# Turns of the cached K rows in layer 1: later places in the order, behind the additions of products

## The chip, the cores and the metric

The kernel runs on one core of a Trainium2 chip. The metric is the device time of one execution in microseconds (us), as the median of several runs. Beside the timed runs stands one execution that was recorded by the hardware profiler; all times inside the kernel come from it. Its engines are named PE (TensorE: matmuls, with PEld for the loads of its stationary operand), DVE (VectorE), ACT (ScalarE), POOL (GpSimd) and SP (SyncE, which here only issues DMAs).

## The reference

A trunk of two layers over a prompt of 512 tokens and a sample group of 8 sequences with 16 new tokens each (640 rows of 1024). Layer 0 is a gated MLP and is not touched. Layer 1 projects q, k, v and z for 16 heads of 128, lets the prompt attend to itself and the sample rows attend to 256 cached rows and themselves, with a bias from cumulative forget values, and gates the result with silu(z). For the sample group:

```python
k = jnp.concatenate([k_cache.astype(k_new.dtype), k_new], axis=1)
v = jnp.concatenate([v_cache.astype(v_new.dtype), v_new], axis=1)
s = jnp.einsum('bqhd,bkhd->bhqk', q, k).astype(jnp.float32) * scale
s = s + cT[:, :, P:, None] - cT[:, :, None, :]
s = jnp.where(mask, s, -jnp.inf)
p = jax.nn.softmax(s, axis=-1).astype(v.dtype)
return jnp.einsum('bhqk,bkhd->bqhd', p, v).reshape(B, T, H * dh)
```

The cached K (8 sequences, 256 rows, 16 heads, 128 values, f32) must stand transposed in memory, with the 128 values on the partitions, before the scores can be computed.

## The kernel before, in words

**Work on PE.** Every f32 matrix is split into a high and a low part, and a product is three matmuls (`mm3`, lines 271 to 273). The projections of layer 1 use Strassen's scheme of seven products for a 2 by 2 block (`seven_products`, from line 556): each of the seven has four `mm3` with 320 columns and ends in one of four PSUM banks. The first product is copied out by ScalarE (line 571); VectorE adds the others to partial sums (lines 573, 575, 578), and four times an addition completes a quarter of the output (`total`, line 562). PE can run ahead of these additions only as far as banks are free.

**Layer 1.** Heads are worked on in eight pairs. The loop over p from 0 to 6 runs four projections in each pass: z of pair p, then v, k and q of pair p+1, 28 `mm3` each. `interleave` counts 0.441 for each `mm3`, so that a projection is 12.35 and a pass 49.4 of its units, and puts the pieces of attention in at given times: scores, turn, values and gate of the prompt heads (`prompt_times`) and of two groups of four sample sequences (`sample_times`), and the loads and turns of cached data. The last pair's attention is spread over project_z(7) and the first half of the output projection (`out_steps` in `tail`).

**Cached K.** `load_k(p, bg, hh)` brings the rows of one head hh of pair p for one group bg of four sequences, 512 KB, into `kraw` by four DMAs of 128 KB, one for each quarter of 32 partitions, issued by SP (line 124). It puts 32 by 32 blocks where they are to be turned. `turn_k(p, bg, hh)` turns them with four transposes on VectorE (line 1051) into `kt[:, hh]`. There is one `kraw` and one `kt` for the two heads: a load can start only when the turn before it has read `kraw`, and a turn can write `kt` only when the sample scores of the group before have read it. `new_k` adds the new rows to `kt` (GpSimd, line 1055). Then the scores of the group are computed on PE (line 1073). A pair has four turns: group 0 head 0, group 0 head 1, group 1 head 0, group 1 head 1; each is followed by the load for the next.

**What sets the order.** The program is traced in the order that `interleave` gives, and the framework then orders the instructions of each engine itself: it runs the program through a simulated timeline and lets an instruction whose operands are ready there pass others that were traced before it. On the chip each engine then works its list off in that order, so an instruction that waits holds up what stands behind it. `queued(...)` limits this: every instruction traced inside it on the named engine is ordered behind the instruction kept in `behind`, without a wait of its own. `behind["dve"]` is set by `total`, so in layer 1 it is the latest traced addition that completed a quarter of a projection.

**Other DMAs of a pass.** SP also issues the loads of cached V, the stores of k (16 DMAs, behind the transposes of `store_k`, line 920) and v (5), the masks and biases and two stores of y. The weights of layer 1 are loaded by GpSimd's queue (line 122).

Of the kernel before, what the change touches and what calls it, by code (L numbers as in the profile page):

```python
# [32 lines left out]
PAST = 256  # L33
# [24 lines left out]
def hybrid_trunk(tc, x_prompt, x_sample, ck, cv, clf, p_prompt, p_sample, norm_pre, norm_post,  # L58
                 g_win, ln_g, ln_b, w_s, b_s, g_wout, f_win, b_f, f_wout, w_proj, w_gate, consts,
                 y_p, y_s, st_v, fk_p, fv_p, fl_p, fk_s, fv_s, fl_s):  # L60
    nc = tc.nc
# [28 lines left out]
    def r1(o, n, p=P):  # L90
        return R1[:p, o:o + n]
# [11 lines left out]
    def bank(lst=(0, 1, 2, 3, 4, 5, 6, 7)):  # L103
        return PB[ring(("bank", lst), lst)]
# [15 lines left out]
    def dma(out, in_, queue=None):  # L120
        if queue is not None:
            queue.dma_start(out=out, in_=in_)
        else:
            behind["sp"] = nc.sync.dma_start(out=out, in_=in_)  # L124

    @contextmanager
    def queued(*engines):

        with ExitStack() as stack:
            for e in engines:  # L130
                stack.enter_context(tc.issue_after(behind[e].ins))
            yield
# [223 lines left out]
    def interleave(steps, pieces):  # L356


        now, todo = 0.0, sorted(pieces, key=lambda x: x[0])
        for took in steps:  # L360
            now += took
            while todo and todo[0][0] <= now:
                todo.pop(0)[1]()
        for _, piece in todo:
            piece()
# [97 lines left out]
    for p in range(4):  # L463
# [3 lines left out]
        out = [bank((0, 1, 2, 3, 4, 5, 6, 7)) for _ in range(NT)]  # L467
# [88 lines left out]
    def seven_products(into, done, partial=None):  # L556

        m1, u2, u3 = partial or (into(0, 0), into(0, 1), into(1, 0))
        rights = (quarter(0, 0), right_sum(1), quarter(0, 1), right_sum(0), quarter(1, 1), quarter(1, 0), right_sum(2))

        def total(i, j, a, b):
            behind["dve"] = nc.vector.tensor_tensor(out=into(i, j), in0=a, in1=b, op=ALU.add)  # L562
            done(i, j, into(i, j))

        for n, (w, right) in enumerate(zip(seven_left(), rights)):
            o = bank(UZ)[:, :HT]
            for k in range(4):
                mm3(o, (w[0][:, k], w[1][:, k]), (right[0][:, k], right[1][:, k]), k == 0, k == 3)
                yield 0.441
            if n == 0:  # L570
                nc.scalar.activation(out=m1, in_=o, func=AF.Copy)
            elif n == 1:
                nc.vector.tensor_tensor(out=u2, in0=m1, in1=o, op=ALU.add)
            elif n == 2:
                nc.vector.tensor_tensor(out=u3, in0=u2, in1=o, op=ALU.add)  # L575
            elif n == 3:
                total(1, 1, u3, o)
                nc.vector.tensor_tensor(out=u2, in0=u2, in1=o, op=ALU.add)
            elif n == 4:
                total(0, 1, u2, o)  # L580
            elif n == 5:
                total(0, 0, m1, o)
            else:
                total(1, 0, u3, o)
# [276 lines left out]
    def both(o, i):  # L861
        return r1(o + i * TOK, TOK)
# [7 lines left out]
    def kn_of(h):  # L870
        return both(o_k, h % 2)[:, 512:]
# [29 lines left out]
    def turn_v(p, i):  # L901

        v = v_of(p)
        b = bank(ATT)
        for t in range(4):
            nc.tensor.transpose(out=b[:, t * P:(t + 1) * P], in_=both(o_vk, i)[:, t * P:(t + 1) * P], identity=ident)
        nc.scalar.activation(out=v[:, :4, i * P:(i + 1) * P], in_=b.rearrange("p (t n) -> p t n", t=4), func=AF.Copy)
        if i:
            b = bank(ATT)
            for z in range(2):  # L910
                nc.tensor.transpose(out=b[:, z * P:(z + 1) * P], in_=both(o_vk, z)[:, 512:], identity=ident)
            nc.scalar.activation(out=v[:, 4], in_=b[:, :256], func=AF.Copy)
            for t in range(NT):
                store_v(p, t)
# [30 lines left out]
    def project_q(p):  # L945

        def done(i, j, c):
            if j == 1:
                nc.scalar.activation(out=qpads[:, i, :, i, :], in_=both(o_q, i)[:, 512:].rearrange("p (b q) -> p b q", b=NB), func=AF.Copy)

        yield from seven_products(lambda i, j: both(o_q, i)[:, HALF[j]], done)

    def project_z(p):

        def done(i, j, c):
            th = r1(o_vk + 3 * HT, HT)
            nc.scalar.activation(out=th, in_=c, func=AF.Tanh, scale=0.5)
            nc.vector.scalar_tensor_tensor(out=c, in0=th, scalar=1.0, in1=c, op0=ALU.add, op1=ALU.mult)

        yield from seven_products(lambda i, j: both(o_z, i)[:, HALF[j]], done, [r1(o_vk + z * HT, HT) for z in range(3)])  # L960

    def project(*parts):
        for part in parts:
            yield from part
# [3 lines left out]
    def w0_of(h):  # L968
        return tri if h % 2 else SF[:, 2048:2560] if h < 14 else r1(o_raw, 512)

    def load_w0(h):
        dma(w0_of(h), c_sc[h].partition_broadcast(P))
# [59 lines left out]
    kraw = r1(o_K, 1024).rearrange("p (b n) -> p b n", b=4)  # L1032
    kt = r1(o_KT, 2176).rearrange("p (h b k) -> p h b k", h=2, b=4)
    vv = r1(o_V, 2048).rearrange("p (b t n) -> p b t n", b=4, t=2)

    def load_k(p, bg, hh):
        for qd in range(4):
            d = slice(qd * 32, (qd + 1) * 32)
            dma(kraw[d].rearrange("p b (c d) -> p (b c) d", d=32),
                ck[0, 4 * bg:4 * bg + 4, :, 2 * p + hh, d].rearrange("b (c j) d -> j (b c) d", j=32))  # L1040

    def load_v(p, bg):
        for z in range(2):
            b = 4 * bg + 2 * z
            dma(vv[:, 2 * z:2 * z + 2].rearrange("p b t n -> p (b t) n"),
                cv[0, b:b + 2, :, 2 * p:2 * p + 2, :].rearrange("b (t k) h d -> k (b t) (h d)", k=P))

    def turn_k(p, bg, hh):

        for bl in range(4):  # L1050
            nc.vector.transpose(out=kt[:, hh, bl, :PAST], in_=kraw[:, bl])  # L1051

    def new_k(p, bg):
        for hh in range(2):
            nc.gpsimd.tensor_copy(out=kt[:, hh, :, PAST:], in_=kn_of(2 * p + hh)[:, 64 * bg:64 * bg + 64].rearrange("p (b k) -> p b k", b=4))
# [61 lines left out]
    def prompt_times(h, t0, step):  # L1117

        setup, scores, turn, values = prompt_pieces(h)
        res = [(t0 - step + 0.1, setup)]  # L1120
        for i in range(4):
            for after, f in ((0, scores), (7.5, turn), (12.5, values)):
                res.append((t0 + step * i + after, lambda f=f, i=i: f(i)))
        return res

    def sample_times(p, bg, t0):
        masks, scores, turn, values, gate = sample_pieces(p, bg)
        return [(t0 - 10, masks), (t0, scores), (t0 + 7.5, turn), (t0 + 12.5, values), (t0 + 17.5, gate)]
# [17 lines left out]
    def attention_pieces(p, step, s1):  # L1146

        s0, t0 = 5, 4
        pieces = sample_times(p, 0, s0) + sample_times(p, 1, s1)
        pieces += [(s0 + 3, lambda: turn_k(p, 1, 0)), (s0 + 3.1, lambda: load_k(p, 1, 1)), (s0 + 15.5, lambda: turn_k(p, 1, 1)),  # L1150
                   (s0 + 15.6, lambda: new_k(p, 1)), (s0 + 13.5, lambda: load_v(p, 1)), (t0 - 3, lambda: load_w0(2 * p + 1))]
        for hh in range(2):
            pieces += prompt_times(2 * p + hh, t0 + 4 * step * hh, step)
        if p < 7:
            pieces += [(s0 + 15.7, lambda: load_k(p + 1, 0, 0)), (s1 + 13.5, lambda: load_v(p + 1, 0)),
                       (t0 + 4 * step if p < 6 else 48, lambda: load_w0(2 * p + 2))]
        return pieces

    def next_keys(p, t, t_new):

        return [(t, lambda: turn_k(p, 0, 0)), (t + 0.1, lambda: load_k(p, 0, 1)), (t + 10, lambda: turn_k(p, 0, 1)),
                (t + 10.1, lambda: load_k(p, 1, 0)), (t_new, lambda: new_k(p, 0))]

    sums = []

    def sums_of_h():
# [3 lines left out]
    interleave(project_k0(), [(1.0, forget_sums), (4.0, lambda: load_k(0, 0, 0)), (6.0, lambda: load_w0(0)), (6.1, lambda: load_v(0, 0))])  # L1170
    split(*quarter(0, 1), sums[0])
    nc.gpsimd.memset(r1(o_qp, 512), 0.0)
    interleave(project_q(0), [(0.2, lambda: turn_k(0, 0, 0)), (0.3, lambda: load_k(0, 0, 1)), (10.0, lambda: turn_k(0, 0, 1)),
                              (10.1, lambda: load_k(0, 1, 0)), (10.2, lambda: new_k(0, 0))])
    for p in range(7):
        pieces = attention_pieces(p, 4.8, 24.7) + next_keys(p + 1, 31.0, 42.0)
        pieces += [(26.0, lambda p=p: turn_v(p + 1, 0)), (27.0, lambda p=p: turn_v(p + 1, 1))]
        interleave(project(project_z(p), project_v(p + 1), project_k(p + 1), project_q(p + 1)), pieces)
        store_y(p)
# [4 lines left out]
    pieces = attention_pieces(7, 5.2, 24.7)  # L1184
# [39 lines left out]
```

## Time and profile before

| | us |
|---|---|
| median of 3 runs | 1323.46 |
| lowest and highest of them | 1320.18 to 1323.74 |
| the profiled execution | 1320.38 |
| its span, first to last instruction | 1318.6 |
| PE busy | 1285.0 |
| DVE busy | 952.4 |
| ACT busy | 588.6 |
| POOL busy | 345.5 |

The profile's page gives busy time, share and instructions of each engine, the span in slices, the DMA queues, the chain of work that ended last, and groups of instructions with their busy time, the mean of one, the idle time of the engine just before them and what ended that idle time. Times in the timeline count from the start of the span; a row is start, length, engine, line, operation, output<-input, shapes and count, and in brackets the idle time before it and its releaser. A row with SPq is DMA issue by SP. PE is a pipeline whose matmuls overlap, so its busy time is the time with any matmul under way. The table of stretches gives for each the busy time and count of each engine, the granted clock of PE (1.00 is the full clock), the share of the DMA engines that was busy, and GB/s.

### The profile page before, as it was taken

What the parts mean: (1) busy time and instruction counts of PE and PEld (TensorE: products, weight loads), DVE (VectorE), ACT (ScalarE), POOL (GpSimd) and SP (SyncE); (2) the same over time, 40 slices, a digit from 0 to 9 for tenths busy, and PEclk for the clock granted to TensorE, in tenths of its full rate; (3) what the DMA queues carried; (4) which work ended last, traced back from release to release, by engine and by line L of the source; (5) the groups of instructions that cost most, each with busy time, mean ns of one, the idle gap of its engine ahead of it and who ended that gap; (6) DMA issues with size and microseconds to landing.
All of it is one profiled execution on the core that took longest, in us unless ns stands there. A gap on an engine that the chain in (4) does not pass through costs nothing.

```text
span 1318.6 us, 21116 instructions
## 1 busy us (share of the span) xinstructions
PE 1285.0 (97%) x7873; PEld 1148.3 (87%) x7873; DVE 952.4 (72%) x1888; ACT 588.6 (45%) x1062; POOL 345.5 (26%) x308
## 2 busy tenths in 40 slices
PE   9999999999999999998979899999989999999998
PEld 6888999999988888886869899999889999888887
DVE  7744999999834455987758797978677887644543
ACT  5434555444535333453425354545444454535431
POOL 1012454543000100343323444444343430000100
PEclk9999999999999999998989999999989999999999
DMA  6432443332324113457777667677787757742211
GB/s 226 133 107 64 122 124 113 94 95 72 128 96 160 65 48 118 113 117 149 151 156 141 172 151 173 150 174 153 128 156 153 182 141 222 260 140 73 71 57 56
DMA packets 276441, 171.53 MB, mean 130 GB/s; under 512 B 188721, under 2 KB 238689, under 8 KB 276338
## 3 DMA queue, kind: packets, MB, share of 16 engines
q1 hardware_dynamic: 267554, 138.46, 37.8%
q0 software_dynamic: 8640, 31.46, 12.6%
q8 instruction: 62, 1.02, 0.3%
q14 instruction: 41, 0.34, 0.1%
q10 hardware_dynamic: 144, 0.26, 0.1%
HBM read 148.55 MB, written 21.59 MB: 129 GB/s over the span
## 4 chain that ended last, share of the span: by engine, by line
PE 81%; DVE 8%; DMA 5%; SPq 3%; issue 2%; ACT 1%; POOL 0%; DVEq 0%; ACTq 0%
PE pb L271 23%; PE pb L273 23%; PE pb L272 23%; DMA R<-in_cache_fox_k 4%; SPq L124 3%; PE pb L1026 2%; DVE W L289 2%; DVE R L1051 2%; PE pb L1073 1%; PE pb L315 1%; PE pb L594 1%; PE pb L1099 1%; PE pb L1019 1%; DVE R L1013 1%; PE pb L893 1%
## 5 line engine op out<-in xcount | busy, mean ns | idle before, releaser
L271 PE MATMUL pb<-A,W 128*128 128x320 f32 (+1 forms) x752 | 245.3, 326 | 5.8 <-DVE R L562 3.4
L273 PE MATMUL pb<-A,W 128*128 128x320 f32 (+1 forms) x752 | 235.8, 314 | 0.0
L272 PE MATMUL pb<-A,W 128*128 128x320 f32 (+1 forms) x752 | 235.4, 313 | 0.0
L271 PE MATMUL pb<-W,A 128*128 128x512 f32 x520 | 204.8, 394 | 0.7 <-ACT A L288 0.7
L289 DVE TENSOR_TENSOR W<-RAW,W 128x1024 fp32r<-128x1024 f32 (+1 forms) x126 | 151.2, 1202 | 73.6 <-ACT W L288 71.0
L273 PE MATMUL pb<-W,A 128*128 128x512 f32 x520 | 203.5, 394 | 0.6 <-DVE A L289 0.6
L272 PE MATMUL pb<-W,A 128*128 128x512 f32 x520 | 203.9, 392 | 0.1
L288 ACT ACTIVATE W<-RAW 128x1024 fp32r<-128x1024 f32 (+1 forms) x126 | 120.1, 953 | 102.9 <-PE pb L273 47.6
L271 PEld LDWEIGHTS pb<-A,W 128*128 128x128 f32 x752 | 143.4, 191 | 14.4 <-issue 6.8
L272 PEld LDWEIGHTS pb<-A,W 128*128 128x128 f32 x752 | 143.5, 191 | 1.2 <-issue 0.9
L273 PEld LDWEIGHTS pb<-A,W 128*128 128x128 f32 x752 | 143.1, 190 | 1.1 <-issue 0.8
L210 POOL TENSOR_TENSOR sff<-RAW 128x512 f32<-128x512 f32 x46 | 60.9, 1325 | 229.4 <-DVE W L292 77.5
L271 PE MATMUL pb<-tbf,W 128*128 128x320 f32 x360 | 117.7, 327 | 0.2 <-DVE R L575 0.2
L273 PEld LDWEIGHTS pb<-W,A 128*128 128x128 f32 x520 | 98.0, 189 | 20.8 <-DVE A L289 0.9
L301 POOL TENSOR_TENSOR SML<-SML 128x1 f32<-128x1 f32 x25 | 18.5, 741 | 372.7 <-DVE SML L299 368.0
L271 PEld LDWEIGHTS pb<-W,A 128*128 128x128 f32 x520 | 98.2, 189 | 20.3 <-ACT A L288 1.1
L272 PEld LDWEIGHTS pb<-W,A 128*128 128x128 f32 x520 | 98.0, 189 | 20.0 <-DVE W L289 0.4
L273 PE MATMUL pb<-tbf,W 128*128 128x320 f32 x360 | 112.9, 313 | 0.0
L272 PE MATMUL pb<-tbf,W 128*128 128x320 f32 x360 | 112.5, 312 | 0.0
L562 DVE TENSOR_TENSOR R<-R,pb 128x320 f32<-128x320 f32 x184 | 86.5, 478 | 17.8 <-PE pb L273 16.7
L1051 DVE STREAM_TRANSPOSE R<-R 128x256 f32<-128x256 f32 x128 | 47.7, 416 | 54.2 <-DMA R<-in_cache_fox_k 46.9
L1010 ACT ACTIVATE R<-R,SML 128x128 f32<-128x128 f32 (+1 forms) x64 | 35.9, 561 | 112.4 <-DVE SML L1009 112.4
(266 smaller groups left out, 2833.0 us busy)
## 6 DMA issues: line engine op xcount, KB each, us to landing
RAW<-in_fox_w_in POOLq DMA_DIRECT2D x46, 512.0 KB, 7.0
RAW<-in_gmlp_w_in SPq DMA_DIRECT2D x40, 512.0 KB
R<-in_cache_fox_v SPq DMA_DIRECT2D x32, 512.0 KB
R<-in_cache_fox_k SPq DMA_DIRECT2D x128, 128.0 KB
RAW<-in_gmlp_w_out SPq DMA_DIRECT2D x16, 512.0 KB
RAW<-in_ple_w_gate SPq DMA_DIRECT2D x16, 512.0 KB
RAW<-in_fox_w_out SPq DMA_DIRECT2D x16, 512.0 KB
R<-in_fox_w_in POOLq DMA_DIRECT2D x14, 512.0 KB, 6.7
```

Of the source, the lines that this page charges most:

```text
L124: behind["sp"] = nc.sync.dma_start(out=out, in_=in_)
L210: nc.gpsimd.tensor_tensor(out=o, in0=a, in1=b, op=op)
L271: nc.tensor.matmul(out, lh, rh, start=start, stop=False)
L272: nc.tensor.matmul(out, lh, rl, start=False, stop=False)
L273: nc.tensor.matmul(out, ll, rh, start=False, stop=stop)
L288: nc.scalar.activation(out=hi, in_=src, func=AF.Copy)
L289: nc.vector.tensor_tensor(out=lo, in0=src, in1=f(hi), op=ALU.subtract)
L301: nc.gpsimd.tensor_tensor(out=q, in0=t, in1=mhalf, op=ALU.pow)
L562: behind["dve"] = nc.vector.tensor_tensor(out=into(i, j), in0=a, in1=b, op=ALU.add)
L1010: nc.scalar.activation(out=pr[:, :n], in_=pr[:, :n], func=AF.Exp, bias=nm, accum_out=sm)
L1026: nc.tensor.matmul(O[:, d], v[:, j, hh * P:(hh + 1) * P], pt[:, j * P:(j + 1) * P], start=(j == 0), stop=(j == i))
L1051: nc.vector.transpose(out=kt[:, hh, bl, :PAST], in_=kraw[:, bl])
```

## The change

`turn_k` is traced inside `queued("dve")`, so its transposes are ordered behind the latest addition that completed a quarter of a projection. The times of the turns in a pass change from 8, 20.5, 31 and 41 to 10, 22.6, 34 and 46, about 12.4 units apart (49.4 / 4), and the loads and `new_k` that belong to them move along; the sample scores of group 1 move from 24.7 to 26.0, and with them the pieces that are timed by `s1` (mask, turn, values, gate, and the load of the next V). The same is done to the turns in project_q(0). For the last pair the turns move too, while its scores of group 1 stay at 24.7. No instruction is added or taken away.

```diff
     def turn_k(p, bg, hh):
 
-        for bl in range(4):
-            nc.vector.transpose(out=kt[:, hh, bl, :PAST], in_=kraw[:, bl])
+        with queued("dve"):
+            for bl in range(4):
+                nc.vector.transpose(out=kt[:, hh, bl, :PAST], in_=kraw[:, bl])
...
-        pieces += [(s0 + 3, lambda: turn_k(p, 1, 0)), (s0 + 3.1, lambda: load_k(p, 1, 1)), (s0 + 15.5, lambda: turn_k(p, 1, 1)),
-                   (s0 + 15.6, lambda: new_k(p, 1)), (s0 + 13.5, lambda: load_v(p, 1)), (t0 - 3, lambda: load_w0(2 * p + 1))]
+        pieces += [(s0 + 5, lambda: turn_k(p, 1, 0)), (s0 + 5.1, lambda: load_k(p, 1, 1)), (s0 + 17.6, lambda: turn_k(p, 1, 1)),
+                   (s0 + 17.7, lambda: new_k(p, 1)), (s0 + 13.5, lambda: load_v(p, 1)), (t0 - 3, lambda: load_w0(2 * p + 1))]
...
-            pieces += [(s0 + 15.7, lambda: load_k(p + 1, 0, 0)), (s1 + 13.5, lambda: load_v(p + 1, 0)),
+            pieces += [(s0 + 17.8, lambda: load_k(p + 1, 0, 0)), (s1 + 13.5, lambda: load_v(p + 1, 0)),
...
-        return [(t, lambda: turn_k(p, 0, 0)), (t + 0.1, lambda: load_k(p, 0, 1)), (t + 10, lambda: turn_k(p, 0, 1)),
-                (t + 10.1, lambda: load_k(p, 1, 0)), (t_new, lambda: new_k(p, 0))]
+        return [(t, lambda: turn_k(p, 0, 0)), (t + 0.1, lambda: load_k(p, 0, 1)), (t + 12, lambda: turn_k(p, 0, 1)),
+                (t + 12.1, lambda: load_k(p, 1, 0)), (t_new, lambda: new_k(p, 0))]
...
-    interleave(project_q(0), [(0.2, lambda: turn_k(0, 0, 0)), (0.3, lambda: load_k(0, 0, 1)), (10.0, lambda: turn_k(0, 0, 1)),
-                              (10.1, lambda: load_k(0, 1, 0)), (10.2, lambda: new_k(0, 0))])
+    interleave(project_q(0), [(0.2, lambda: turn_k(0, 0, 0)), (0.3, lambda: load_k(0, 0, 1)), (12.0, lambda: turn_k(0, 0, 1)),
+                              (12.1, lambda: load_k(0, 1, 0)), (12.2, lambda: new_k(0, 0))])
     for p in range(7):
-        pieces = attention_pieces(p, 4.8, 24.7) + next_keys(p + 1, 31.0, 42.0)
+        pieces = attention_pieces(p, 4.8, 26.0) + next_keys(p + 1, 34.0, 46.2)
```

## The prediction

> **What bounds the kernel now.** I read the page first. Its head, the engines' busy times, the chain of work that ended last and the group of the moved instructions:
>
> ```profile
> span 1318.6 us, 21116 instructions
> ...
> PE 1285.0 (97%) x7873; PEld 1148.3 (87%) x7873; DVE 952.4 (72%) x1888; ACT 588.6 (45%) x1062; POOL 345.5 (26%) x308
> ...
> PE 81%; DVE 8%; DMA 5%; SPq 3%; issue 2%; ACT 1%; POOL 0%; DVEq 0%; ACTq 0%
> ...
> L1051 DVE STREAM_TRANSPOSE R<-R 128x256 f32<-128x256 f32 x128 | 47.7, 416 | 54.2 <-DMA R<-in_cache_fox_k 46.9 <-DMA out<-R 7.2
> ```
>
> PE sets the time: 97% busy, 81% of the chain, and only 1318.6 - 1285.0 = 33.6 us without a matmul. The last line is the turns of cached K: VectorE stood idle 54.2 us in front of them, nearly all for their own load. A turn that waits holds everything queued behind it on VectorE, also the additions that empty PE's banks of products. So the question is how much of the 54.2 us reaches PE.
>
> For that I cut layer 1 at the points where the first product of projection z is copied out by line 571, one row for each pass of the loop over pairs. The columns are the stretch, its length, busy time (and count) of PE, PEld, DVE, ACT, POOL, then the granted clock, the DMA share and GB/s:
>
> ```profile
> 587.40:667.40 80.00, 75.40 (x496) 64.46 (x496) 60.31 (x159) 33.56 (x67) 31.84 (x32) 0.96 0.75 143
> 667.40:753.20 85.80, 73.06 (x515) 67.58 (x514) 59.17 (x150) 32.52 (x66) 31.25 (x29) 0.92 0.74 155
> 753.20:820.70 67.50, 67.50 (x509) 63.73 (x508) 58.53 (x149) 33.05 (x67) 29.17 (x29) 1.00 0.71 166
> 820.70:888.40 67.70, 67.70 (x508) 63.74 (x508) 58.05 (x149) 33.00 (x67) 29.14 (x29) 1.00 0.73 157
> 888.40:960.90 72.50, 69.32 (x507) 64.83 (x507) 57.51 (x149) 32.55 (x66) 27.24 (x28) 0.98 0.76 150
> 960.90:1035.60 74.70, 70.60 (x509) 65.87 (x508) 58.24 (x149) 33.01 (x67) 31.87 (x30) 0.95 0.79 164
> 1035.60:1104.60 69.00, 68.43 (x512) 64.39 (x512) 55.75 (x147) 32.55 (x65) 21.37 (x22) 1.00 0.66 163
> ```
>
> Seven passes with the same work; two of them have PE busy without a gap and take 67.5 and 67.7 us. That is PE's floor for a pass, 67.6. Over it lie 12.4, 18.2, 0, 0, 4.9, 7.1 and 1.4 us, 44.0 in all. In the passes that are over, the granted clock is below 1.00 too.
>
> The timeline of PE shows where it stood still, with the idle time and its releaser in brackets:
>
> ```profile
> 687.07 0.47 PE L1019 MATMUL pb<-CST,R 128*128 128x128 f32 x1 [7.02 <-DVE R L1013]
> ...
> 730.00 0.49 PE L1026 MATMUL pb<-R 128*128 128x128 f32 x2 [3.83 <-DVE R L1028]
> ...
> 937.79 0.49 PE L1026 MATMUL pb<-R 128*128 128x128 f32 x2 [3.18 <-DVE R L1028]
> ...
> 980.84 0.63 PE L271 MATMUL pb<-A,W 128*128 128x320 f32 x1 [3.43 <-DVE R L562]
> ```
>
> VectorE released all four. Its own timeline tells why it was late (613.94 is a wait in the first pass, 677.92 one for a store, the others are turns):
>
> ```profile
> 613.94 1.42 DVE L1051 STREAM_TRANSPOSE R<-R 128x256 f32<-128x256 f32 x4 [4.87 <-DMA R<-in_cache_fox_k]
> ...
> 677.92 0.49 DVE L575 TENSOR_TENSOR R<-R,pb 128x320 f32<-128x320 f32 x1 [6.67 <-DMA out<-R]
> ...
> 685.75 1.10 DVE L1051 STREAM_TRANSPOSE R<-R 128x256 f32<-128x256 f32 x3 [7.27 <-DMA R<-in_cache_fox_k]
> ...
> 726.73 1.42 DVE L1051 STREAM_TRANSPOSE R<-R 128x256 f32<-128x256 f32 x4 [7.22 <-DMA out<-R]
> ...
> 863.48 1.42 DVE L1051 STREAM_TRANSPOSE R<-R 128x256 f32<-128x256 f32 x4 [3.48 <-DMA R<-in_cache_fox_k]
> ...
> 934.51 1.43 DVE L1051 STREAM_TRANSPOSE R<-R 128x256 f32<-128x256 f32 x4 [6.57 <-DMA R<-in_cache_fox_k]
> ...
> 978.59 0.77 DVE L1051 STREAM_TRANSPOSE R<-R 128x256 f32<-128x256 f32 x2 [6.41 <-DMA R<-in_cache_fox_k]
> ```
>
> Each of the four stops of PE goes with a turn that waited 6.4 to 7.3 us. The wait of 3.48 at 863.48 lies in a pass on the floor: up to about 3.5 us PE has products and other work to cover it.
>
> **What a stop costs.** After each of these stops the clock is at half. The same table for those stretches:
>
> ```profile
> 682.60:692.80 10.20, 4.32 (x16) 3.88 (x17) 7.05 (x22) 2.40 (x5) 1.27 (x1) 0.50 0.80 192
> 730.40:733.80 3.40, 3.40 (x14) 3.40 (x14) 3.37 (x12) 1.83 (x4) 1.36 (x4) 0.50 0.63 99
> 938.60:942.00 3.40, 3.40 (x16) 2.75 (x19) 3.37 (x11) 1.92 (x4) 1.36 (x3) 0.50 0.49 76
> 979.50:986.40 6.90, 5.57 (x22) 4.79 (x26) 6.90 (x21) 3.35 (x6) 1.99 (x3) 0.51 0.58 80
> ```
>
> Half of PE's busy time in them is lost. With the idle time: 7.02 + 4.32/2 = 9.2 at 687; 3.83 + 1.7 = 5.5 at 730; 3.18 + 1.7 = 4.9 at 938, which is that pass's whole excess of 4.9; 3.43 + 2.8 = 6.2 at 981, of 7.1. Together 25.8 us hang on four turns.
>
> The dips last 3.4, 3.4, 6.9 and 10.2 us: one, two and three times 3.4. The Trainium skill, "TensorE: Matmul & The Clock Gate", Part 1, says that the clock is halved once PE was idle for a window of about 3.4 us and comes back after a busy one. The lengths agree; that a stop of 3.18 already halved the clock does not. By that rule stops that are shortened well under a window, but stay, would give back the half clock alone (2.2 + 1.7 + 1.7 + 2.8 = 8.4 us, so 1312), where the sum below takes whole stops.
>
> **The change, part by part.** *The edge.* No instruction is added; 128 transposes get an order behind the latest traced addition of a product on VectorE (line 562). With the new times 10, 22.6, 34 and 46 in a pass of 49.4, that addition is the second of the four in z, v, k and q. Today the turns stand ahead of it, as the timeline of VectorE in a pass on the floor shows (line 562 is an addition of products):
>
> ```profile
> 824.61 1.10 DVE L1051 STREAM_TRANSPOSE R<-R 128x256 f32<-128x256 f32 x3
> ...
> 829.16 0.47 DVE L562 TENSOR_TENSOR R<-R,pb 128x320 f32<-128x320 f32 x1
> ...
> 854.49 0.43 DVE L1051 STREAM_TRANSPOSE R<-R 128x256 f32<-128x256 f32 x1
> ...
> 867.74 0.48 DVE L562 TENSOR_TENSOR R<-R,pb 128x320 f32<-128x320 f32 x1
> ...
> 869.93 0.48 DVE L562 TENSOR_TENSOR R<-R,pb 128x320 f32<-128x320 f32 x1
> ...
> 881.81 0.49 DVE L562 TENSOR_TENSOR R<-R,pb 128x320 f32<-128x320 f32 x1 [1.68 <-PE pb L273]
> ...
> 896.85 0.47 DVE L562 TENSOR_TENSOR R<-R,pb 128x320 f32<-128x320 f32 x1
> ```
>
> 829.16 is the second addition of z, 867.74 and 869.93 are the second and third of k, 881.81 is the second of q, 896.85 of the next z. The turn at 824.61 must move behind 829.16, the one that ends at 854.49 + 0.43 = 854.92 behind 867.74, and the one of 863.48, quoted above, behind 881.81: by 5, 13 and 18 us.
>
> *The spacing.* SP issues the loads; four of its rows are needed here and below:
>
> ```profile
> 673.87 2.80 SPq L124 DMA_DIRECT2D R<-in_cache_fox_k  x1
> ...
> 871.32 12.40 SPq L124 DMA_DIRECT2D out<-R  x16
> ...
> 966.52 9.86 SPq L124 DMA_DIRECT2D R<-in_cache_fox_k  x4
> ...
> 1115.88 9.18 SPq L124 DMA_DIRECT2D r2c_t<-y_sc  x12
> ```
>
> kraw has one buffer, so a load starts when the turn before it ends. Today the second turn of a group follows as soon as its load is expected: after the turn that ends at 854.92 comes the one whose wait ends at 863.48, 8.6 us later. The load of 966.52 ends the wait at 978.59, 12.1 us later. Behind the second additions the turns stand 881.81 - 867.74 = 14.1 us (k to q), 896.85 - 881.81 = 15.0 (q to z) and, over the two steps from 829.16 to 867.74, 19.3 on average apart. Less 1.5 us for the turn itself, 12.6 to 17.8 are left for loads that take 8.6 to 12.1. So the waits of the later passes should fall to between 0 and 2, under the cover of 3.5.
>
> *What goes.* The stops at 730, 938 and 981 go whole: 5.5 + 4.9 + 6.2 = 16.6. The one at 687 is mixed. VectorE first waited 6.67 us for a store, which PE covered (it stood still only from 687.07 - 7.02 = 680.05), then 7.27 for the turn. Behind the second addition of z this turn no longer blocks that addition, but its load was late in itself: its last quarter was issued at 673.87 and took until 685.75. If it stays so late, some 4 to 5 us of wait remain (an estimate: 7.27 less what now goes first); I take 8.0 of the 9.2, between 0 and 9.2.
>
> *What stays.* The first pass's 12.4 us: its turns run a projection behind their nominal places already (the one of 613.94 is traced in the projection before 587.40), so the edge binds nothing there. I take 0, with up to 4.9 (a stop like that at 938) as a gain if the order that follows happens to help. The rest of pass 2 and pass 7 (5.0 and 1.4) I leave as well.
>
> *What is added.* A turn of 1.42 us now sits between the second and the third addition, which are 869.93 - 867.74 = 2.2 us apart; the delay is under the 3.5 that PE covers: nothing, and 1.42 a turn in 28 turns if that cover were gone (40). Sample scores of the second group wait for a turn that moves from 20.5 to 22.6 and are themselves traced 1.3 later; PE has the rest of the projection to run ahead of them. In the tail it is not free. The last pair's third turn moves behind the second addition of z, so the load after it meets the twelve loads that SP issues from 1115.88 on. The turn behind it may then wait in the tail, with the softmax and splits of out_steps queued behind it on VectorE: 0 to 6.2 (the stop at 981); I take 2.
>
> Sum: 16.6 + 8.0 - 2 = 22.6 us. The profiled execution took 1320.4 us (1.8 outside its span), so 1297.8, in round numbers **1298**. The three runs have a median of 1323.5 and reach from 1320.2 to 1323.7; the profiled one lies at their lower end, and against the median the forecast is 25 us or 1.9%.
>
> **The rivals.** *Slower: the load behind the stores of k.* The turn in k comes between its second and third addition, and behind the third and fourth SP has to issue 16 stores, which took 12.40 us from 871.32. If quarters of the load for the next turn fall behind them, they leave at about 884 and land 2 to 12 us later (978.59 less the end of the issue at 976.38, and 685.75 - 673.87), while the turn in q stands at about 882. It would wait 4 to 14 us, in each of seven passes, with the next two additions of q behind it. It decides from a wait of about 6.5 us, where the loss for a pass reaches 22.6/7 = 3.2. At the price of a wait of 7.2 (5.5): 1297.8 + 7 x 5.5 = **1336**. For it: the load of 673.87 left its last quarter to the second pass, long after the turn before. Against: the four issues are ready 1.5 us after 867.74, the first store only after the third addition at 869.93 and a transpose. [...]
>
> *Half.* SP's issue itself is stretched (9.86 us for four at 966.52), and with the DMA engines 66 to 79% busy a load could still be late now and then. Half of the gain: **1309**.
>
> *Nothing.* The change does not do what it says: the edge binds nowhere, as in the first pass: **1320**. Against it: the turn of 824.61 is ahead of 829.16 and cannot stay there.
>
> *All.* The first passes come to the floor too: 1320.4 - 44.0 = **1276**. Against: the first load's lateness isn't touched.
>
> **How the numbers follow.** A measurement of this kernel can tell about 0.3% (4 us) from no change. Chances: forecast 0.55, half 0.18, all 0.08, nothing 0.08, slower 0.11. Faster by over 0.3%: 0.55 + 0.08 + 0.16 of the half case = 0.79; within: 0.08 + 0.02 = 0.10; slower: 0.11. The forecast's own bounds: all of 687, nothing in the tail and 5 in the first pass give 1298 - 1.2 - 2 - 4.9 = 1290; nothing of 687 and the whole tail price give 1298 + 8 + 4 = 1310. Leaving out "slower" and "all" (0.19), the range goes from 1287, a little under the first bound, to the 1320 of no change.
>
> **What would show it.** Right: idle time in front of the turns (line 1052 in the changed file) falls from 54 us to under 20; passes 5 and 6 come to 67.5 to 69; no half clock in passes 3 to 7; the transposes stand behind the second addition in each projection. Wrong: half clock in q of each pass (the slower rival), waits in front of the turns as long as today, with the same passes over the floor, or passes above 70 us with VectorE waiting on something else.

## The result and the profile after

| | before | after |
|---|---|---|
| median, us | 1323.01 | 1343.64 |
| lowest to highest of 4 runs | 1320.18 to 1323.74 | 1342.86 to 1346.08 |
| the profiled execution | 1320.38 | 1343.14 |
| its span | 1318.6 | 1341.3 |

The four runs of before are the three of above and one more. The ratio after to before is 1.0163, with a 95% interval of 1.0143 to 1.0183: slower by 20.6 us, where 25 us of gain had been forecast. The page of the changed kernel has, in the places shown before, its span, the engines' busy times, the chain of waits, and two groups of instructions:

```profile
span 1341.3 us, 21141 instructions
...
PE 1294.5 (97%) x7873; PEld 1149.7 (86%) x7873; DVE 971.5 (72%) x1888; ACT 583.9 (44%) x1062; POOL 350.7 (26%) x308
...
PE 63%; DVE 19%; DMA 10%; issue 3%; SPq 2%; ACT 1%; DVEq 0%; ACTq 0%
...
L1052 DVE STREAM_TRANSPOSE R<-R 128x256 f32<-128x256 f32 x128 | 46.0, 410 | 4.5 <-DMA R<-in_cache_fox_k 2.6 <-PE pb L1074 1.3 <-issue 0.4
...
L1071 DVE TENSOR_TENSOR R<-R,CST 128x16 f32<-128x16 f32 x16 | 4.2, 261 | 53.6 <-DMA R<-cs_sc 53.6
```

The edit did just what it says: the 54.2 us that VectorE stood in front of the turns are 4.5. But 53.6 us stand in front of another instruction, the addition to the sample mask `Wc` (line 1071; 0.26 us of work, 16 times). In the kernel before it had none, as its group there says:

```profile
L1070 DVE TENSOR_TENSOR R<-R,CST 128x16 f32<-128x16 f32 x16 | 3.5, 219 | 0.0
```

VectorE's waits after, with what is waited for, us in total, how often, and the longest:

```profile
DVE R L1071 <- DMA R<-cs_sc: 53.6, 11, 9.4
...
DVE R L562 <- DMA y_sc<-R: 21.9, 3, 11.0
```

A second new wait: an addition of products that stands until a store of y has left. The stretches, cut and read as in the prediction:

```profile
587.40:670.80 83.40, 74.06 (x484) 65.73 (x482) 58.91 (x154) 32.82 (x64) 31.74 (x32) 0.92 0.75 148
670.80:745.70 74.90, 72.46 (x529) 65.95 (x528) 60.67 (x154) 33.33 (x70) 28.10 (x29) 1.00 0.77 161
745.70:817.60 71.90, 69.54 (x507) 63.63 (x507) 60.65 (x150) 31.96 (x66) 30.01 (x28) 1.00 0.65 148
817.60:891.80 74.20, 69.73 (x508) 63.65 (x507) 61.70 (x149) 31.92 (x66) 30.85 (x29) 1.00 0.68 148
891.80:971.80 80.00, 72.63 (x509) 66.53 (x508) 61.74 (x148) 31.98 (x67) 30.19 (x29) 0.96 0.69 130
971.80:1052.70 80.90, 71.67 (x507) 65.56 (x507) 62.61 (x150) 31.83 (x66) 32.04 (x29) 0.96 0.75 157
1052.70:1124.90 72.20, 69.22 (x507) 63.63 (x506) 59.56 (x146) 32.06 (x65) 24.78 (x23) 1.00 0.62 148
```

The second pass gained 10.9 us; all others lost: 3.4, 4.4, 6.5, 7.5, 6.2 and 3.2. Together 537.5 instead of 517.2, so 20.3 of the span's 22.7 us; what lies behind the passes took 216.4 instead of 214.0.

**Where the mask's wait comes from.** `Wc` has one buffer, so its load can start only when the scores of the group before have been read (line 1077 after). The addition is traced with the next scores, but the framework puts it far ahead of them. VectorE and SP after, in pass 4:

```profile
856.78 0.43 DVE L1077 CUSTOM_DVE_ANT_0 R<-pb,R 128x272 f32<-128x272 f32 x1
...
865.13 0.18 DVE L1071 TENSOR_TENSOR R<-R,CST 128x16 f32<-128x16 f32 x1 [6.24 <-DMA R<-cs_sc]
...
870.28 0.47 DVE L562 TENSOR_TENSOR R<-R,pb 128x320 f32<-128x320 f32 x1
870.68 0.43 DVE L1052 STREAM_TRANSPOSE R<-R 128x256 f32<-128x256 f32 x1
```

```profile
857.24 0.60 SPq L124 DMA_DIRECT2D R<-cs_sc  x1
```

The load goes out at 857.24 and the addition is the sixth instruction behind the reading of the scores, so VectorE waits 6.24 us for it. The turn is where the change put it, behind an addition of line 562 (870.28). The same place in the kernel before, on VectorE and on SP:

```profile
864.82 0.13 DVE L1070 TENSOR_TENSOR R<-R,CST 128x16 f32<-128x16 f32 x1
```

```profile
854.95 6.29 SPq L124 DMA_DIRECT2D R<-in_cache_fox_k  x4
861.28 0.66 SPq L124 DMA_DIRECT2D R<-cs_sc  x1
```

There the scores were read at 854.85 and the mask's addition was the twentieth instruction behind that, right behind the turn of 863.48, which the prediction shows with its wait of 3.48. While VectorE waited for that load, the mask landed too. The turn's wait did not only hold VectorE up, it covered a second wait. The mask's load itself also took longer after, 7.9 us from its issue, where it had landed within 3.5 before; why, no run shows.

**Where the store's wait comes from.** SP after, at the start of pass 6; then VectorE's waits and PE's stops after, in passes 5 and 6:

```profile
972.82 0.38 SPq L124 DMA_DIRECT2D y_sc<-R  x1
973.30 12.55 SPq L124 DMA_DIRECT2D R<-in_cache_fox_k  x4
985.95 1.93 SPq L124 DMA_DIRECT2D y_sc<-R  x1
```

```profile
906.46 0.49 DVE L562 TENSOR_TENSOR R<-R,pb 128x320 f32<-128x320 f32 x1 [7.91 <-DMA y_sc<-R]
...
945.04 0.17 DVE L1071 TENSOR_TENSOR R<-R,CST 128x16 f32<-128x16 f32 x1 [7.92 <-DMA R<-cs_sc]
...
990.17 0.49 DVE L562 TENSOR_TENSOR R<-R,pb 128x320 f32<-128x320 f32 x1 [10.99 <-DMA y_sc<-R]
```

```profile
907.40 0.64 PE L271 MATMUL pb<-A,W 128*128 128x320 f32 x1 [3.49 <-DVE R L578]
...
945.87 0.55 PE L1092 MATMUL pb<-CST,R 128*128 128x128 f32 x3 [2.58 <-DVE SML L1006]
...
991.11 0.64 PE L271 MATMUL pb<-A,W 128*128 128x320 f32 x1 [7.28 <-DVE R L578]
```

In the kernel before, SP had issued the second store ahead of the load of 966.52:

```profile
959.69 0.46 SPq L124 DMA_DIRECT2D y_sc<-R  x1
```

With the new times the four loads of cached K stand between the two stores of y on SP, which needed 12.55 us to issue them. The second store left at 985.95, and the first finished quarter of z, which overwrites y, waited for it. Waits of 7.91, 7.92 and 10.99 us on VectorE stopped PE for 3.49, 2.58 and 7.28 us: what PE has in hand lasts 3.7 to 5.3 us. Behind the last stop the clock is at half, as in the prediction's table (the columns are the same):

```profile
988.90:995.80 6.90, 4.69 (x19) 4.65 (x20) 5.62 (x17) 3.04 (x6) 0.85 (x1) 0.52 0.32 74
```

Half of PE's 4.69 us in it is lost, 2.3. With the stop of 7.28 that is 9.6 of the 13.3 us that pass 6 lies over the floor.

The Trainium skill, "DMA: Bandwidth & Descriptors", Issuing engines are not separate DMA queues, says that the time to start a DMA is usually small beside the DMA itself. Most loads of K in these passes agree: the four that follow at 993.57 took SP 2.32 us. But the four of 973.30 took 12.55 us, longer than the whole way of such a load elsewhere (8.6 us in the prediction); the measurement decides.

### The profile page after: what moved, and what is told of

It reads as the page before. It is cut to its first block, busy times and chain, and to the rows that moved or that the text cites. A ratio compares the mean times of both kernels' runs of the same rounds, so it can differ in the third digit from the quotient of the medians.

```text
span 1341.3 us, 21141 instructions
## 1 busy us (share of the span) xinstructions
PE 1294.5 (97%) x7873; PEld 1149.7 (86%) x7873; DVE 971.5 (72%) x1888; ACT 583.9 (44%) x1062; POOL 350.7 (26%) x308
## 4 chain that ended last, share of the span: by engine, by line
PE 63%; DVE 19%; DMA 10%; issue 3%; SPq 2%; ACT 1%; DVEq 0%; ACTq 0%
PE pb L271 19%; PE pb L273 19%; PE pb L272 19%; DMA R<-cs_sc 5%; DVE W L289 4%; SPq L124 2%; DVE R L1052 2%; DVE W L292 2%; DMA R<-in_cache_fox_k 2%; DVE R L562 2%; DMA y_sc<-R 1%; PE pb L315 1%; PE pb L1026 1%; DVE R L958 1%; PE pb L594 1%
## 5 line engine op out<-in xcount | busy, mean ns | idle before, releaser
L271 PE MATMUL pb<-A,W 128*128 128x320 f32 (+1 forms) x752 | 243.3, 324 | 13.4 <-DVE R L578 11.1
L289 DVE TENSOR_TENSOR W<-RAW,W 128x1024 fp32r<-128x1024 f32 (+1 forms) x126 | 159.3, 1265 | 74.6 <-ACT W L288 69.9
L562 DVE TENSOR_TENSOR R<-R,pb 128x320 f32<-128x320 f32 x184 | 86.0, 477 | 25.6 <-DMA y_sc<-R 21.9
L289 DVE TENSOR_TENSOR A<-R,A 128x640 fp32r<-128x640 f32 (+1 forms) x42 | 34.4, 853 | 59.7 <-ACT A L288 59.7
```

Of the source, the lines that this page charges most:

```text
L271: nc.tensor.matmul(out, lh, rh, start=start, stop=False)
L289: nc.vector.tensor_tensor(out=lo, in0=src, in1=f(hi), op=ALU.subtract)
```

## The experiments

Theory A was: the loss is these two waits, the mask's first. The first rival: the loss comes from the moved turns themselves. Each later expectation names its own rivals. The ratios stand against the kernel before, run on the same chip.

**The mask's addition tied as well.** After, with

```diff
-            nc.vector.tensor_tensor(out=Wc[:, PAST:], in0=Wc[:, PAST:], in1=CST[:, C_M16:C_M16 + TS], op=ALU.add)
+            with queued("dve"):
+                nc.vector.tensor_tensor(out=Wc[:, PAST:], in0=Wc[:, PAST:], in1=CST[:, C_M16:C_M16 + TS], op=ALU.add)
```

> The changed kernel, with the addition to the mask of the sample scores (line 1071 there) also tied behind the latest addition of products, so that it stands a projection later on VectorE. Theory A (the wait that went from the turns came back at the mask: 53.6 us of VectorE waiting on the mask's load in the changed kernel, about 34 us of it felt by PE by the passes over the floor of 67.6): waits on the mask fall from 53.6 us to under 10, passes 3 and 7 come from 71.9 and 72.2 to 68 to 69, the stops at the store of y stay; 1308 to 1318 us. Rival B (the turns themselves, 1.4 us each between the second and third addition of every projection, cost the 4.4 us a pass): the mask's wait goes, the passes stay at 71 to 72; 1338 to 1344 us. Rival C (only the store of y behind the K load costs): no change beyond 5 us.

Measured: 1315.3 us, 0.9940 (0.9924 to 0.9956). No wait for the mask is left, and the time falls by 28.3 us under after. Passes 3 and 7 come to 68.9 and 68.4 us, as theory A said and not the 71 to 72 of rival B. The other wait stays (VectorE's waits):

```profile
DVE R L562 <- DMA y_sc<-R: 20.5, 3, 10.0
```

**The second store of y ahead of the load.** After, with `load_k(p + 1, 1, 0)` taken out of `next_keys` and traced behind the stores:

```diff
-                (t + 12.1, lambda: load_k(p, 1, 0)), (t_new, lambda: new_k(p, 0))]
+                (t_new, lambda: new_k(p, 0))]
...
         store_y(p)
+        with queued("sp"):
+            load_k(p + 1, 1, 0)
```

> The changed kernel, with the load of K for group 1 head 0 of the next pair issued behind the two stores of y instead of between them. Theory A: the waits of z's first finished quarter on the store of y (2.98, 7.91 and 10.99 us in passes 4 to 6) go, and with them the half clock at 907 and 989; passes 5 and 6 come from 80.0 and 80.9 to about 72; 1323 to 1330 us. Rival C (the store of y is the whole loss): 1300 to 1310 us. Rival D (z waits for something else that ends at the same time): passes 5 and 6 stay at 80.

Measured: 1347.26 us, 1.0193 (1.0152 to 1.0235). The waits for the store are gone but for 0.7 us, and nothing is gained, where 14 to 21 us had been expected: passes 5 and 6 take 78.7 and 82.7 us. VectorE's waits, and the place of pass 6 on SP and VectorE:

```profile
DVE R L1071 <- DMA R<-cs_sc: 73.2, 13, 10.2
```

```profile
981.35 7.64 SPq L124 DMA_DIRECT2D R<-in_cache_fox_k  x1
989.09 0.85 SPq L124 DMA_DIRECT2D R<-cs_sc  x1
```

```profile
992.14 0.18 DVE L1071 TENSOR_TENSOR R<-R,CST 128x16 f32<-128x16 f32 x1 [10.23 <-DMA R<-cs_sc]
```

The mask's load now stands behind the load of K, and its addition took over nearly the whole wait: 53.6 + 21.9 = 75.5 us in the changed kernel, 73.2 here.

**Both edits.**

> Both of the former edits to the changed kernel. Theory A: all passes after the first come to 67.5 to 69.5 us, no half clock after the second pass; 1285 to 1300 us, below the kernel before. Rival B (turns between the additions cost 4.4 us a pass): passes of 71 to 72, 1315 to 1325 us.

Measured: 1313.2 us, 0.9925 (0.9905 to 0.9944), 13 us above the upper end of what was expected. Passes 3 to 5 are even at 68.8 to 68.9 us. At the start of pass 6 the wait went on again, to a turn: 9.1 us, the longest of 20.3 that turns waited for their loads. One wait of 3.5 us for the store stays, in pass 2.

**The edge alone, the times alone, and the mask's edit in the kernel before.** The first is before with `queued` around the turns; the second is after without it; the third is before with the mask's edit.

> The kernel before, with the turns tied behind the latest additions and the old times. Theory A: the order on VectorE keeps the mask's addition right behind a turn, so it has the turn's load as cover, but on SP the K load now stands ahead of both stores of y, so z waits for them as in the changed kernel or more (3 to 11 us a pass); turns wait less than the 54 us before; 1320 to 1345 us. Rival E (the edge alone makes the loss, by holding the turns late whatever the times): 1338 to 1350 us with few waits on the store of y.

Measured: 1338.54 us, 1.0119 (1.0095 to 1.0143), with 34.8 us of waits for the mask, 18.9 for the store, 20.4 for turns. The time lies in the ranges of both theory A and rival E; of the mechanisms, the store's wait came as theory A said, but its cover for the mask did not.

> The changed kernel without the tie: the new times alone. Its order on VectorE keeps the mask's addition right behind the second turn of each group, and on SP both stores of y stand ahead of the K load. Theory A (the loss needs the mask's addition to stand without a turn ahead of it): no waits on the mask, waits on turns of 30 to 60 us in all as before; 1312 to 1330 us. Rival F (the later sample work that comes with the new times costs by itself): 1335 us or more.

Measured: 1321.31 us, 0.9981 (0.9967 to 0.9996), no wait for the mask, 53.9 us in front of turns.

> The kernel before, with only the mask's addition tied behind the latest addition of products. Theory A (in the kernel before, the mask arrives in the cover of a turn's wait, so it costs nothing there): the same turns wait as long as before, passes of 67.5 to 68.5 where there were such, 1317 to 1330 us, no difference beyond 0.5%. Rival H (a mask tied late helps whatever the turns do): under 1312 us.

Measured: 1322.11 us, 0.9996 (0.9974 to 1.0019), 63.5 us in front of turns. So the edge alone makes some 15.6 of the 20.6 us of loss; the times without it change the time by 0.2%, and the rest comes only with both. And the mask's early place cost nothing as long as a turn's wait stood ahead of it.

**The turns of a group later.** The two edits together, and the turns of group 1 moved from 10 and 22.6 to about 14 and 24, those of group 0 to 35 and 47, sample scores to 27:

```diff
-        pieces += [(s0 + 5, lambda: turn_k(p, 1, 0)), (s0 + 5.1, lambda: load_k(p, 1, 1)), (s0 + 17.6, lambda: turn_k(p, 1, 1)),
+        g0, g1 = (9, 19) if p < 7 else (5, 17.6)
+        pieces += [(s0 + g0, lambda: turn_k(p, 1, 0)), (s0 + g0 + 0.1, lambda: load_k(p, 1, 1)), (s0 + g1, lambda: turn_k(p, 1, 1)),
...
-        pieces = attention_pieces(p, 4.8, 26.0) + next_keys(p + 1, 34.0, 46.2)
+        pieces = attention_pieces(p, 4.8, 27.0) + next_keys(p + 1, 35.0, 47.2)
```

> The kernel with both edits (mask tied, K load behind the stores of y), with the turns of group 1 at 14 and 24 and those of group 0 at 35 and 47, so that the turn in z comes some 6 us later. Theory A: the wait of 9.1 us of that turn in pass 6, where the load is slow, falls under 4 us and is covered; pass 6 from 77.8 to 69 to 73; 1303 to 1310 us. Rival G (pass 6 is held up by the weights themselves, which move slowly there): pass 6 stays at 75 or more; 1311 to 1317 us.

Measured: 1299.3 us, 0.9822 (0.9797 to 0.9848): faster than both kernels, and than expected. The stretches of passes 1 to 7, from its profiled execution of 1303.8 us:

```profile
587.30:667.60 80.30, 75.84 (x492) 64.36 (x491) 60.63 (x159) 33.84 (x67) 33.12 (x32) 0.96 0.75 141
667.60:743.40 75.80, 70.54 (x520) 65.03 (x519) 60.61 (x149) 33.53 (x68) 28.33 (x29) 1.00 0.77 173
743.40:810.80 67.40, 67.40 (x508) 63.56 (x508) 59.75 (x149) 33.15 (x67) 28.63 (x29) 1.00 0.75 167
...
945.60:1019.90 74.30, 70.57 (x509) 65.33 (x507) 59.82 (x149) 32.97 (x66) 28.57 (x29) 0.95 0.77 167
1019.90:1087.10 67.20, 67.20 (x507) 63.33 (x506) 57.10 (x147) 32.73 (x65) 21.76 (x22) 1.00 0.67 159
```

Passes 3, 4, 5 and 7 lie on PE's floor. Above it are only 1, 2 and 6. The expected gain came only in part: the turn's wait at the start of pass 6 fell from 9.1 to 3.7 us, but the pass took 74.3 us, 3.5 less than with both edits, where 69 to 73 were expected. The larger part, 6.3 us, came in passes 3, 4, 5 and 7, of which the expectation said nothing. One wait for the store of y stays, 8.2 us in pass 2.

**No loads of K.** Both edits, at the change's times, and only the first load of cached K is made; all others are left out, so the sample attention works on old keys. One run.

> The kernel with both edits, with all loads of cached K but the first left out; the turns work on what lies there, and everything else stays. Theory A: no turn waits, the stores of y and the masks are served at once; passes of 68.5 to 69.5 in pass 3 to 7, 1288 to 1302 us. If the weights' packets at the start of pass 6 still take some 420 to 450 ns on average (200 to 250 in pass 3), they are slow by themselves; if they fall to 250, the K load made them slow. Rival B (turns between additions cost more than 1 us a pass in themselves): passes 3 to 5 stay at 68.9.

Measured: 1300.06 us, in theory A's range, with passes 3 to 5 at the 68.9 us of rival B. Two rows of its table, passes 3 and 6:

```profile
738.40:807.30 68.90, 68.90 (x509) 63.90 (x508) 62.21 (x149) 33.13 (x67) 29.63 (x29) 1.00 0.50 133
...
945.00:1013.80 68.80, 68.80 (x507) 63.81 (x507) 63.83 (x149) 32.80 (x66) 30.49 (x29) 1.00 0.64 145
```

In passes 3 to 7 VectorE waits for no DMA at all (in pass 2 it waits 5.2 us for a store of y), yet a pass takes 68.8 to 68.9 us, 1.4 to 1.5 over the 67.4 of the version with later turns, without any gap of PE. The records show where that time goes. In pass 3 two of PE's groups of attention matmuls, sample scores and sample values, are split by transposes of the prompt's attention; with later turns they are whole. The split scores without loads, and the whole ones with later turns:

```profile
770.86 0.66 PE L1077 MATMUL pb<-R 128*32 128x272 f32 x6
771.45 0.66 PE L1019 MATMUL pb<-CST,R 128*128 128x128 f32 x4
772.03 1.10 PE L1077 MATMUL pb<-R 128*32 128x272 f32 x10
```

```profile
776.72 1.12 PE L1075 MATMUL pb<-R 128*32 128x272 f32 x16
```

The busy time of these sample scores alone in pass 3 (32 matmuls; the number behind the stretch's length), in the same order:

```profile
738.40:807.30 68.90, 2.89 (x32) 0.94 (x32) 1.00 0.50 133
```

```profile
743.40:810.80 67.40, 2.25 (x32) 0.83 (x32) 1.00 0.75 167
```

The values of the sample groups take 2.75 instead of 2.14 us, and the transposes between them (line 1019) 3.60 instead of 3.48: 1.4 us in all. So this goes with the order of the matmuls on PE, not with a wait of VectorE, and rival B's price of the turns themselves is not shown by it. The version with later turns still has turns between the additions of v, k and q and loses nothing by them. Why a split group takes longer, and whether the turns or the scores, which also came later, changed the order, was not tried.

Pass 6 is on a level with pass 3: its excess elsewhere comes with the loads. The weights are slower there all the same. The DMA issues of pass 3 and, below, of the first 30 us of pass 6, with count, KB each and median us from issue to landing:

```profile
RAW<-in_fox_w_in POOLq DMA_DIRECT2D x6, 512.0 KB, 6.4
...
R<-in_fox_w_in POOLq DMA_DIRECT2D x2, 512.0 KB, 6.8
```

```profile
RAW<-in_fox_w_in POOLq DMA_DIRECT2D x3, 512.0 KB, 7.6
...
R<-in_fox_w_in POOLq DMA_DIRECT2D x1, 512.0 KB, 11.2
```

7.6 instead of 6.4 us for the one half and 11.2 instead of 6.8 for the other, with no load of K on the way. What the expectation asked of the packets has its answer too: by the queue's share of the DMA engines (24.9% of 68.9 us for 1152 packets, 52.3% of 30 us for 546) a packet of weights took some 238 ns in pass 3 and 460 at the start of pass 6. The loads of K are not what makes them slow.

**Two variants of the best version.** First, it without the edit that puts the store ahead. Then, with the stores of y issued by ScalarE (`dma(y_sc[2 * p + hh], y_of(2 * p + hh), nc.scalar)`), and `load_k(p + 1, 1, 0)` at the same place but not tied behind them.

> The kernel with the mask tied and the later turns (14, 24, 35, 47), but with the K load between the two stores of y again, as in the changed kernel. Theory A (the store of y behind a K load is a loss of its own wherever the K load is slow): waits on the store of y come back in passes 2 and 6, 5 to 10 us each, and pass 6 goes from 74.3 to 75 to 78; 1303 to 1310 us. Rival G (the order of those stores never mattered, the later turns alone made the gain): 1298 to 1301 us.

Measured: 1308.07 us, 0.9887 (0.9866 to 0.9907), with 18.9 us of waits for the store in two waits, in passes 2 and 6 as theory A said, where the best version has one of 8.2. The same edit that gained nothing by itself is worth 8.8 us here.

> The kernel with the mask tied and the later turns, with the stores of y issued by ScalarE's queue, so that they stand behind nothing on SP, and the K load not ordered behind them. Theory A (what z waits for is the place in SP's queue): no wait on the store of y over 4 us, 1293 to 1300 us. Rival I (the DMA engines themselves are the bound there, whatever queue issues): waits on the store of y in passes 2 and 6 of 5 to 10 us stay, 1300 to 1308 us.

Measured: 1301.35 us, 0.9831 (0.9812 to 0.9850): not to be told from the version that it varies. Theory A's 1293 to 1300 was missed and neither mechanism holds whole: pass 6 comes to 67.2 us there, but a store still holds VectorE up by 7.0 us in pass 2, and passes 1 and 5 take 83.2 and 70.4.

## Why the prediction was wrong

**The bound: right.** PE sets the time and VectorE's waits stop it. PE's floor of 67.6 us came again (67.4 with later turns). The cover of 3.5 us was the lower end: 3.7 to 5.3. One row was misread: not every pass over the floor has a clock below 1.00, the seventh (69.0 us) has 1.00.

**The edge and the spacing: right.** The turns moved behind the second additions, and their loads were there in time: 4.5 us of waits in all, where "between 0 and 2" in the later passes was said.

**What goes: the step that failed.** It took the stops at 938 and 981 as removed whole, 11.1 us, once the turn's wait was gone. After, PE stopped for 3.49 us at 907, 2.58 at 946 and 7.28 at 991, and passes 5 and 6 lost 7.5 and 6.2 us instead. Two things were missing. The step never asked what stood next behind the turn on VectorE: the mask's addition, whose group showed 0.0 us of waiting and so looked harmless, though its load left SP right behind the load of K (issue from 861.28, that of K until 861.24) and came in under the wait of 3.48. And the step said nothing of what the moved load of K passes on SP: the second store of y. The mask's part is measured: 28.3 us between after and after with the mask tied. The store's part depends on what else waits: nothing while the mask stands behind the same loads, 2.1 with the mask tied (1315.3 to 1313.2, within the intervals of both), 8.8 with the turns late. In pass 2 the step came close: 13.5 us were forecast (8.0 at 687, 5.5 at 730), 10.9 came, though with waits for the mask of 5.2 and 4.0 us in place of the turns'.

**What stays: nearly right.** The first pass kept its excess and got longer: 12.4 us before, 15.8 after, with a wait of 9.4 for the mask in it. Its 80.3 us in the best version shows that nothing here reached it.

**What is added.** A turn between additions was put at nothing a pass, as VectorE's delay is under what PE covers. That holds for the delay, but the new order has a price elsewhere, which this term left out: 1.4 us a pass on PE, some 10 us over seven passes if each pays as pass 3 does in the version without loads. The tail was put at 2 us and took 2.4, by luck: no turn waited for its load there, where the term rested on such a wait.

**The rivals.** The slower case had a chance of 0.11, and its 1336 is near 1343.6, but its mechanism did not come: the turns, those in q among them, wait 4.5 us in all. The loss came by the sign named last, "VectorE waiting on something else". The time of "nothing" came only without the edge (1321.3), which is not that rival's mechanism. The 1312 of stops that are shortened but stay did not come either: there were new ones.

**What stays open.** At the start of pass 6, in several kernels the instruction that needs a DMA waits 9 to 11 us: an addition behind the store in after (10.99) and with the mask tied (10.0), the mask's with the store ahead (10.23), a turn with both (9.1). With later turns it is 3.7, and with the stores on ScalarE none. Weights land late there even without loads of K; why was not tried. Nor were the 80 us of the first pass taken apart.

## What to carry to other kernels

Before a wait is taken away, read on that engine's timeline what stands directly behind it and when that instruction's own data was sent for: a wait of 0.0 in a group can be one that another wait covers. Of a DMA that is moved, list what it now stands ahead of on its issuing queue, small loads and stores above all, and who waits for those. A fix that gains nothing alone can be worth its price once the wait that covers it is gone, so try the edits together too. And where an engine gets slower without a gap, compare the order of its instructions: here the same matmuls cost 1.4 us more a pass when their groups were split.

## What was not expected of the hardware

SP's issue of four loads of K (128 KB each) takes 2.1 to 13.9 us in these runs. With the mask tied, two loads that follow each other on SP:

```profile
952.68 9.54 SPq L124 DMA_DIRECT2D R<-in_cache_fox_k  x4
...
972.83 2.13 SPq L124 DMA_DIRECT2D R<-in_cache_fox_k  x4
```

Everything behind the first on SP, a mask of 136 KB or a store, leaves that much later. What stretches it is not shown: without the loads of K, SP still took 10.62 us to issue the two stores of y at 661.72.

The length of a stop of PE did not decide alone whether the clock fell. A stop of 2.44 us at 614 in the kernel before was followed by half the clock, one of 3.31 at 685 in the version with later turns was not. Every stop of 3.35 us or more in layer 1 of these traces came with half the clock.
